# RG-LRU gates of a hybrid decoder step: high and low halves stacked in one operand, two products for each block of 64 channels instead of three for each gate

## The chip, the cores and the metric

The kernel runs on one core of a Trainium2 chip. The metric is the device time of one execution in microseconds (us). Engines are named as in the profile: PE (TensorE matmul; PEld is its weight load), DVE (VectorE), ACT (ScalarE), POOL (GpSimd), SP (SyncE, which issues loads). POOL issues the stores.

## The reference

One layer with two parallel head groups, for a prompt of 1024 tokens and for 8 decode rows. Both groups read one projection of the normalised input. What the change touches is the RG-LRU group's gates: the channels (1024) are cut into 16 blocks of 64, and each block has its own 64x64 weights.

```python
xc = conv_b + sum(conv_w[j] * ext[:, j:j + S] for j in range(CONV_W))
blocks = xc.reshape(B, S, NB_A, BW_A)                       # NB_A = 16, BW_A = 64
r = sigmoid(einsum('bsnc,ncd->bsnd', blocks, w_r) + b_r)
i = sigmoid(einsum('bsnc,ncd->bsnd', blocks, w_i) + b_i)
log_a = -LRU_C * r * softplus(-lam)
a = exp(log_a)
u = sqrt(-expm1(2.0 * log_a)) * (i * xc)
...                                                          # h = scan of (a, u) over the tokens
merged = concat[yA * silu(za), yB * silu(zb)]                # yB: mLSTM group
x = x + merged @ w_out
```

## The kernel before

Everything is float32. A product of float32 accuracy is made of parts: `split` writes a high half (a cast to the reduced format `fp32r`, on ACT) and a low half (source minus high, on DVE), and `mm3` adds three products, high by high, low by high and high by low, in one PSUM bank.

The program has three stretches. First the input is normalised, turned and split. Then the input projection runs over 14 units of column pairs (`UNITS`), each of 7 products (`Q_P1` to `Q_P4`, a Strassen-like scheme over 2x2 blocks), each product in two halves of 12 or 24 `mm3` products. Last come the mLSTM chunks (`m_a`, `m_b` ...) and the output projection.

Beside the projection runs a background: after each half product `pop_bg` takes steps from three lists, `bg` (gates' preparation, openings), `rgq` (RG-LRU, one step each time) and `dcq` (decode state). `rg_unit` puts a pair of column blocks into `rgq` once their `x` and `y` columns are stored: each column block `j` has 128 channels on the partitions and two halves `b` of 512 tokens, and `rg_half` gives the steps of one half, so there are 16 half blocks. A pair of column blocks is 4 half blocks and one load step. The last steps are `rg_final`, an empty one and `rg_rows`. When all lists are empty after the last q, k, v unit, `m_start` puts the mLSTM's first steps (`m_first`) into `bg`.

One half block before: `conv1` and `conv2` do the four taps on DVE and split the result `xc` into `xh` and `xl`; `gate_r` and `gate_i` each do one `mm3` on `xh`, `xl` with the weights `ghi`, `glo` of that gate and one tanh on ACT; `decay`, `scan` and `outs` follow on DVE and ACT. The weights stand in `graw` [128, 2, 128]: gate by gate, two 64x64 blocks on the diagonal, zeros elsewhere. Both gates' results go to the one PSUM bank with the tag `s`. The bank with the tag `tr` serves `dec_unit` alone at this time: 8 products of the decode rows and, a step later, their transposes. `rg_dec` does the same gates for the 8 decode rows with plain float32 products. `hb` holds half the biases, [channel, column block, gate].

The instruction order on each engine is made by a scheduler from the program's order and its own readiness estimates, so neighbours may change places.

Of the kernel before, what the change touches and what calls it, by code (L numbers as in the profile page):

```python
# [9 lines left out]
F32 = mybir.dt.float32  # L10
F32R = mybir.dt.float32r
BF16 = mybir.dt.bfloat16
AF = mybir.ActivationFunctionType
ALU = mybir.AluOpType
# [3 lines left out]
P = 128  # L18
T = 1024
HT = 512  # L20
NB = 8
# [8 lines left out]
R_CW, R_CB, R_BR, R_BI, R_LAM, R_GM, R_H0, R_CONV, R_N0, R_END = 0, 4, 5, 6, 7, 8, 9, 17, 41, 49  # L30
# [19 lines left out]
def hymba_kernel(  # L50
# [7 lines left out]
    V, A, G, TE = nc.vector, nc.scalar, nc.gpsimd, nc.tensor  # L58
    ld = nc.sync.dma_start
    stq = nc.gpsimd.dma_start  # L60

    def mm3(out, ah, al, bh, bl, first, last):

        TE.matmul(out, ah, bh, start=first, stop=False, skip_group_check=True)  # L64
        TE.matmul(out, ah, bl, start=False, stop=False, skip_group_check=True)  # L65
        TE.matmul(out, al, bh, start=False, stop=last, skip_group_check=True)  # L66

    def split(hi, lo, src):

        A.copy(hi, src)  # L70
        V.tensor_tensor(lo, src, hi.bitcast(F32), op=ALU.subtract)  # L71
# [7 lines left out]
    def ps(tag, shape):  # L79
        return psp.tile(shape, F32, tag=tag, name=f"ps_{tag}", bufs=NBUF.get(tag, 1))  # L80

    def const(shape, name, dt=F32):
        return cpool.tile(shape, dt, tag=name, name=name)
# [14 lines left out]
    def sg(shape, name, dt=F32):  # L98

        return stg.tile(shape, dt, tag="stg", name=name)  # L100
# [4 lines left out]
    def dconst(shape, name):  # L105

        return dpool.tile(shape, F32, tag=name, name=name)
# [10 lines left out]
    PT = dconst([P, KC, R_END], "PT")  # L118
# [5 lines left out]
    hb = const([P, KC, 2], "hb")  # L124
# [12 lines left out]
    dgr = dconst([P, 2, KC, NB], "dgr")  # L137
# [219 lines left out]
    fp = es_f.enter_context(tc.tile_pool(name="f_start", bufs=1))  # L357
# [161 lines left out]
    es_f = ExitStack()  # L519
    fp = es_f.enter_context(tc.tile_pool(name="f_gates", bufs=1, reuse_waits="tile"))  # L520

    def gates():

        par = ws([R_END, T], "par", F32)
# [22 lines left out]
        fx, ab, lg, z, z2, p = (gx[:, n, :] for n in range(6))  # L547
# [7 lines left out]
        lfd = lg[:, 32:64].rearrange("p (b h) -> p b h", h=NH)  # L555
        V.tensor_scalar(sp2, lg[:, 64:72], -2.0, None, op0=ALU.mult)
        V.tensor_scalar(sp4n, lg[:, 64:72], 4.0, None, op0=ALU.mult)
        V.tensor_scalar(hb, PT[:, :, R_BR:R_BR + 2], 0.5, None, op0=ALU.mult)
        V.tensor_scalar(gm4, PT[:, :, R_GM], 0.25, None, op0=ALU.mult)

        dgm = fp.tile([P, 2, NB, NH], F32, tag="dgm", name="dgm")
# [47 lines left out]
        for half in range(2):  # L609
            pk = ps(("s", "qp")[half], [P, 4, P])  # L610
            for q in range(4):
                c = half * 4 + q
                TE.transpose(pk[:, q, :], stk[:, c * P:(c + 1) * P], idF)
            s = slice(half * 4, half * 4 + 4)
# [20 lines left out]
    fpr = {}  # L635

    def rd_open():

        es_f.close()
        fpr["es"] = ExitStack()  # L640
        fpr["p"] = fpr["es"].enter_context(tc.tile_pool(name="f_rd", bufs=1, reuse_waits="tile"))
        fpr["graw"] = [fpr["p"].tile([P, 2, P], F32, tag=f"graw{i}", name=f"graw{i}") for i in range(2)]
        for t in fpr["graw"]:
            G.memset(t, 0.0)
        rg_gw(0)
        stq(s_conv[0, :, 0:2, :], st_conv[0, :, 1:3, :])
        dec_open()

    rst = {}
# [21 lines left out]
    def rg_unit(jj):  # L671
# [10 lines left out]
        if jj == 3:  # L682
            rgq.extend([rg_final, lambda: None, rg_rows])

    def rg_gw(j):
        if j < KC:
            graw = fpr["graw"][j % 2]
            for n, src in enumerate((w_rgate, w_igate)):
                for two in range(2):
                    s = slice(two * 64, two * 64 + 64)  # L690
                    ld(graw[s, n, s], src[0, 2 * j + two])

    def rg_half(j, b):
        fp = fpr["p"]
        pc = lambda r, n=1: PT[:, j, r:r + n]
        st = {}

        n = 2 * j + b

        def conv1():  # L700
            rg_load(n, True)
            xs = st["xs"] = rst["x", n]
            rg_load(n + 1)
            if b == 0:
                rg_gw(j + 1)
                ghi = fp.tile([P, 2, P], F32R, tag="ghi", name="ghi")
                glo = fp.tile([P, 2, P], F32R, tag="glo", name="glo")
                split(ghi, glo, fpr["graw"][j % 2])
                rst["g", j] = ghi, glo
            st["xc"] = xc = fp.tile([P, HT], F32, tag="xc", name="xc")  # L710
            V.tensor_scalar(xc, xs[:, 3:3 + HT], pc(R_CW + 3), pc(R_CB), op0=ALU.mult, op1=ALU.add)
            for t in (2, 1):
                V.scalar_tensor_tensor(xc, xs[:, t:t + HT], pc(R_CW + t), xc, op0=ALU.mult, op1=ALU.add)

        def conv2():
            xs, xc = st["xs"], st["xc"]
            V.scalar_tensor_tensor(xc, xs[:, 0:HT], pc(R_CW), xc, op0=ALU.mult, op1=ALU.add)
            st["xh"] = fp.tile([P, HT], F32R, tag="xh", name="xh")
            st["xl"] = fp.tile([P, HT], F32R, tag="xl", name="xl")
            split(st["xh"], st["xl"], xc)  # L720
            if b == 1:
                V.tensor_copy(OC[:, j, 1:4], xs[:, HT:HT + 3])

        def gate(g):
            ghi, glo = rst["g", j]
            pg = ps("s", [P, 512])
            mm3(pg, ghi[:, g, :], glo[:, g, :], st["xh"], st["xl"], True, True)
            return pg

        def gate_r():  # L730
            rg_load(n + 1, True)
            pg = gate(0)
            st["rg"] = fp.tile([P, HT], F32, tag="rg", name="rg")
            A.activation(st["rg"], pg, AF.Tanh, scale=0.5, bias=hb[:, j, 0:1])

        def gate_i():
            pg = gate(1)

            st["na"], st["ig"] = (fp.tile([P, HT], F32, tag=t, name=m) for m, t in (("na", "xh"), ("ig", "xl")))
            A.activation(st["ig"], pg, AF.Tanh, scale=0.5, bias=hb[:, j, 1:2])  # L740
            A.activation(st["na"], st["rg"], AF.Tanh, scale=sp2[:, j:j + 1], bias=sp2[:, j:j + 1])
            A.activation(st["rg"], st["rg"], AF.Exp, scale=sp4n[:, j:j + 1], bias=sp4n[:, j:j + 1])
            V.scalar_tensor_tensor(st["ig"], st["ig"], 1.0, st["xc"], op0=ALU.add, op1=ALU.mult)

        def decay():
            rg, na = st["rg"], st["na"]
            V.scalar_tensor_tensor(na, rg, 1.0, na, op0=ALU.add, op1=ALU.mult)
            V.tensor_scalar(rg, na, -1.0, 1.0, op0=ALU.mult, op1=ALU.add)
            V.scalar_tensor_tensor(na, na, 2.0, na, op0=ALU.subtract, op1=ALU.mult)
            A.activation(na, na, AF.Sqrt, scale=-0.25)  # L750

        def scan():
            rg, ig, na = st["rg"], st["ig"], st["na"]
            V.tensor_tensor(ig, ig, na, op=ALU.mult)
            V.tensor_tensor_scan(na, rg, ig, 0.0 if b == 0 else OC[:, j, 0:1], op0=ALU.mult, op1=ALU.add)
            V.tensor_copy(OC[:, j, 0:1], na[:, HT - 1:HT])

        def outs():
            na, zs = st["na"], rst["z", n]
            V.scalar_tensor_tensor(na, na, 0.5, zs, op0=ALU.mult, op1=ALU.mult)  # L760
            mh, ml = sg([P, HT], "rmh", F32R), sg([P, HT], "rml", F32R)
            split(mh, ml, na)
            stq(d_rm[0, j, :, b * HT:(b + 1) * HT], mh.bitcast(F32))
            stq(d_rm[1, j, :, b * HT:(b + 1) * HT], ml.bitcast(F32))
        return [conv1, conv2, gate_r, gate_i, decay, scan, outs]

    def rg_dec(j):

        pc = lambda r, n=1: PT[:, j, r:r + n]
        xc = dxc[:, j, :]  # L770
        cst = PT[:, j, R_CONV:R_CONV + 24].rearrange("p (b t) -> p b t", t=3)
        V.tensor_scalar(xc, dxz[:, 0, j, :], pc(R_CW + 3), pc(R_CB), op0=ALU.mult, op1=ALU.add)
        for t in range(3):
            V.scalar_tensor_tensor(xc, cst[:, :, t], pc(R_CW + t), xc, op0=ALU.mult, op1=ALU.add)
        pg = ps("s", [P, 2, NB])
        for g in range(2):
            TE.matmul(pg[:, g, :], fpr["graw"][j % 2][:, g, :], xc, start=g == 0, stop=True, skip_group_check=True)
        for g in range(2):
            A.activation(dgr[:, g, j, :], pg[:, g, :], AF.Tanh, scale=0.5, bias=hb[:, j, g:g + 1])

    def rg_final():

# [563 lines left out]
    def preps(n):  # L1346
        while state["prep"] < min(n, len(seq)):
            prep(*seq[state["prep"]])
            state["prep"] += 1

    gg = gates()
    bg.extend([lambda: next(gg, None)] * 17 + [rd_open])
    last_u = len(units) - 1
# [62 lines left out]
    for n in range(4, N):  # L1416
        c, h = n // 4, n % 4
# [90 lines left out]
```

## Time and profile before

| | us |
|---|---|
| median of 3 runs | 966.44 |
| the runs | 966.44, 966.21, 969.55 |
| the profiled execution | 970.22 |
| its span, first to last instruction | 968.1 |
| PE, DVE, ACT busy | 941.3, 697.4, 546.1 |
| gate products, first to last start | 143.8 to 535.8 |
| decode rows' gate products (L777), last start | 547.9 |

In rows of the profile, L12 is line 12 of the kernel. A group's row gives line, engine, operation, out<-in by the program's tile names, count, busy time, mean of one in ns, and idle time ahead of it with what ended it. `ps_s` is the PSUM tile of the tag `s`, `ps_tr` that of `tr`. In a row by tile, the three durations are least, median and greatest in ns, then first and last start. A timeline's row begins with start and duration in us. A row of waits gives who waited for whom, us in total, number and the longest.

### The profile page before, as it was taken

What the parts mean: (1) busy time and instruction counts of PE and PEld (TensorE: products, weight loads), DVE (VectorE), ACT (ScalarE), POOL (GpSimd) and SP (SyncE); (2) the same over time, 40 slices, a digit from 0 to 9 for tenths busy, and PEclk for the clock granted to TensorE, in tenths of its full rate; (3) what the DMA queues carried; (4) which work ended last, traced back from release to release, by engine and by line L of the source; (5) the groups of instructions that cost most, each with busy time, mean ns of one, the idle gap of its engine ahead of it and who ended that gap; (6) DMA issues with size and microseconds to landing.
All of it is one profiled execution on the core that took longest, in us unless ns stands there. A gap on an engine that the chain in (4) does not pass through costs nothing.

```text
span 968.1 us, 15367 instructions
## 1 busy us (share of the span) xinstructions
PE 941.3 (97%) x5402; PEld 768.4 (79%) x5402; DVE 697.4 (72%) x1447; ACT 546.1 (56%) x984; POOL 146.5 (15%) x260
## 2 busy tenths in 40 slices
PE   7999989999999999899999999999999999999997
PEld 7797767777787988687889898875667788888886
DVE  6775898988888877777786846686566677676764
ACT  6554456666666756454566744456546366465643
POOL 1111112121212122202212221010200100000020
PEclk9999999999999999999999999999999999999999
DMA  5431447356645455437645453424973754564481
GB/s 191 137 126 43 131 134 271 129 176 196 220 152 196 166 177 172 156 124 242 193 163 167 150 180 95 157 93 154 308 212 98 197 142 128 150 184 140 120 110 49
DMA packets 129314, 153.17 MB, mean 158 GB/s; under 512 B 13750, under 2 KB 107990, under 8 KB 129230
## 3 DMA queue, kind: packets, MB, share of 16 engines
q1 hardware_dynamic: 111510, 96.33, 33.8%
q0 software_dynamic: 17728, 55.87, 16.7%
q8 instruction: 42, 0.69, 0.3%
q14 instruction: 34, 0.28, 0.1%
HBM read 100.59 MB, written 51.65 MB: 157 GB/s over the span
## 4 chain that ended last, share of the span: by engine, by line
PE 43%; DMA 5%; DVE 5%; issue 4%; ACT 1%; POOL 0%; SPq 0%; DVEq 0%; POOLq 0%; ACTq 0%
PE ps_o L66 7%; PE ps_o L64 7%; PE ps_o L65 7%; PE ps_kv L64 5%; PE ps_kv L65 5%; PE ps_kv L66 5%; DMA W<-d_alpha 3%; PE ps_tr L227 1%; PE ps_s L1058 1%; DVE Cl L71 1%; PE ps_qp L64 1%; DVE Cf L1119 1%; DMA rh<-d_rm 1%; PE ps_qp L65 1%; PE ps_qp L66 1%
## 5 line engine op out<-in xcount | busy, mean ns | idle before, releaser
L70 ACT CAST wh<-raw 128x1024 fp32r<-128x1024 f32 x91 | 95.5, 1050 | 74.7 <-PE ps_o L65 24.5
L71 DVE TENSOR_TENSOR wl<-raw,wh 128x1024 fp32r<-128x1024 f32 x91 | 110.9, 1218 | 31.6 <-ACT wh L70 19.4
L64 PE MATMUL ps_kv<-cb_hi,wh 128*128 128x512 f32 x320 | 129.0, 403 | 0.1
L66 PE MATMUL ps_kv<-cb_hi,wl 128*128 128x512 f32 x320 | 126.1, 394 | 0.0
L65 PE MATMUL ps_kv<-cb_lo,wh 128*128 128x512 f32 x320 | 125.9, 393 | 0.0
L64 PE MATMUL ps_o<-cb_hi,wh 128*128 128x512 f32 x240 | 94.7, 394 | 0.0
L66 PE MATMUL ps_o<-cb_hi,wl 128*128 128x512 f32 x240 | 93.9, 391 | 0.0
L65 PE MATMUL ps_o<-cb_lo,wh 128*128 128x512 f32 x240 | 93.7, 390 | 0.0
L64 PEld LDWEIGHTS ps_kv<-cb_hi,wh 128*128 128x128 f32 x320 | 60.4, 189 | 24.8 <-issue 5.5
L66 PEld LDWEIGHTS ps_kv<-cb_hi,wl 128*128 128x128 f32 x320 | 60.5, 189 | 15.7 <-issue 2.5
L65 PEld LDWEIGHTS ps_kv<-cb_lo,wh 128*128 128x128 f32 x320 | 60.6, 189 | 11.9
L66 PE MATMUL ps_o<-wo,ml 128*128 128x512 f32 (+1 forms) x136 | 52.2, 384 | 3.2 <-DVE ml L71 3.1
L64 PE MATMUL ps_kv<-wh,cb_hi 128*128 128x256 f32 x192 | 55.3, 288 | 0.0
L65 PE MATMUL ps_kv<-wl,cb_hi 128*128 128x256 f32 x192 | 54.3, 283 | 0.0
L66 PE MATMUL ps_kv<-wh,cb_lo 128*128 128x256 f32 x192 | 54.3, 283 | 0.0
L64 PE MATMUL ps_o<-wo,rh 128*128 128x512 f32 (+1 forms) x136 | 53.9, 397 | 0.0
L64 PEld LDWEIGHTS ps_o<-cb_hi,wh 128*128 128x128 f32 x240 | 45.1, 188 | 10.8 <-issue 1.7
L66 PEld LDWEIGHTS ps_o<-cb_hi,wl 128*128 128x128 f32 x240 | 45.0, 188 | 10.3 <-issue 0.8
L64 PE MATMUL ps_o<-wo,mh 128*128 128x512 f32 (+1 forms) x136 | 52.9, 389 | 0.0
L65 PE MATMUL ps_o<-wo,rh 128*128 128x512 f32 (+1 forms) x136 | 52.3, 384 | 0.0
L65 PEld LDWEIGHTS ps_o<-cb_lo,wh 128*128 128x128 f32 x240 | 45.1, 188 | 9.0
L66 PE MATMUL ps_o<-wo,rl 128*128 128x512 f32 (+1 forms) x136 | 52.1, 383 | 0.0
(469 smaller groups left out, 2506.9 us busy)
## 6 DMA issues: line engine op xcount, KB each, us to landing
raw<-in_w_in_dram SPq DMA_DIRECT2D x56, 512.0 KB
Cb<-in_state_mlstm_C_dram SPq DMA_DIRECT2D x32, 256.0 KB
out_dram<-Cb POOLq DMA_DIRECT2D x32, 256.0 KB, 4.6
qk<-d_qk SPq DMA_DIRECT2D x32, 256.0 KB
oraw<-in_w_out_dram SPq DMA_DIRECT2D x16, 512.0 KB
d_qk<-s POOLq DMA_DIRECT2D x24, 256.0 KB, 4.2
x<-in_x_prompt_dram SPq DMA_DIRECT2D x8, 512.0 KB
d_x<-s POOLq DMA_DIRECT2D x16, 256.0 KB, 2.9
```

Of the source, the lines that this page charges most:

```text
L64: TE.matmul(out, ah, bh, start=first, stop=False, skip_group_check=True)
L65: TE.matmul(out, ah, bl, start=False, stop=False, skip_group_check=True)
L66: TE.matmul(out, al, bh, start=False, stop=last, skip_group_check=True)
L70: A.copy(hi, src)
L71: V.tensor_tensor(lo, src, hi.bitcast(F32), op=ALU.subtract)
L227: TE.matmul(pz[32 * g:32 * g + 32, :], hnd[:, k, :], raws[u, k // 4][:, k % 4, :], start=k < 4, stop=k >= 4, skip_group_check=True)
L1058: TE.matmul(S, qk[:, 2 + kb, :], qk[:, kb, :], start=kb == 0, stop=kb == 1)
L1119: V.scalar_tensor_tensor(mx["Cf"][h][:, kb, :], mx["Cf"][h][:, kb, :], cs_b[:, h, c:c + 1], kvs[kb], op0=ALU.mult, op1=ALU.add)
```

## The change

- `graw` is filled otherwise: both 64-row halves hold the same weights, and the free index runs over the block first (0 or 1), with the r gate's 64 columns and the i gate's 64 behind it. It is now full, so its two clearing memsets go.
- The input has two operands instead of `xh` and `xl`: operand `n` has the high half of block `n` on that block's own 64 partitions and the low half on the other 64. Four instructions of 64 partitions write them: two casts on ACT in `conv2`, two differences on DVE in a step of their own, `lows`, between `conv2` and the first gate step.
- A product of operand `n` with the stacked weights gives (high + low) times the high weights, for both gates at once: r on the lower 64 partitions of the bank, i on the upper 64. A second adds the low weights. So there are two products for each block and four for a half block, where there were six; the product of low by low comes in addition.
- Block 0 goes to the bank `s`, block 1 to the bank `tr`.
- `gate_out` takes a block's bank apart: tanh of its lower half into the block's 64 partitions of `rg`, tanh of its upper half into those of `ig`. That is four tanh of 64 partitions for a half block instead of two of 128. `hb` is stored to match.
- `rg_dec` does the same: the two halves of `xc` are copied into `dxs`, whose other halves are zero, and there are four small tanh instead of two.
- A half block has 8 steps instead of 7.

```diff
-        V.tensor_scalar(hb, PT[:, :, R_BR:R_BR + 2], 0.5, None, op0=ALU.mult)
+        for n, s in enumerate(LOHI):
+            for m, d in enumerate(LOHI):
+                V.tensor_scalar(hb[d, :, n], PT[s, :, R_BR + m], 0.5, None, op0=ALU.mult)
...
-        for t in fpr["graw"]:
-            G.memset(t, 0.0)
+        fpr["dxs"] = fpr["p"].tile([P, 2, NB], F32, tag="dxs", name="dxs")
+        G.memset(fpr["dxs"], 0.0)
...
+    def gate_out(rg, ig, pg, j, n):
+        for m, t in enumerate((rg, ig)):
+            A.activation(t[LOHI[n]], pg[LOHI[m]], AF.Tanh, scale=0.5, bias=hb[LOHI[m], j, n:n + 1])
...
-                for two in range(2):
-                    s = slice(two * 64, two * 64 + 64)
-                    ld(graw[s, n, s], src[0, 2 * j + two])
+                for s in LOHI:
+                    ld(graw[s, :, n * 64:n * 64 + 64], src[0, 2 * j:2 * j + 2].rearrange("t c d -> c t d"))
...
-            split(st["xh"], st["xl"], xc)
+            st["xx"] = [fp.tile([P, HT], F32R, tag=t, name=t) for t in ("xh", "xl")]
+            for n, s in enumerate(LOHI):
+                x = st["xx"][n]
+                A.copy(x[s], xc[s])
...
+        def lows():
+            for n, s in enumerate(LOHI):
+                x = st["xx"][n]
+                V.tensor_tensor(x[LOHI[1 - n]], st["xc"][s], x[s].bitcast(F32), op=ALU.subtract)
+
+        def gate(n):
+            pg = ps(("s", "tr")[n], [P, 512])
+            for k, w in enumerate(rst["g", j]):
+                TE.matmul(pg, w[:, n, :], st["xx"][n], start=k == 0, stop=k == 1)
             return pg
...
-        return [conv1, conv2, gate_r, gate_i, decay, scan, outs]
+        return [conv1, conv2, lows, gate_a, gate_b, decay, scan, outs]
...
+        for n, s in enumerate(LOHI):
+            V.tensor_copy(dxs[s, n, :], xc[s])
```

`gate_a` and `gate_b` each call `gate` for one block and `gate_out` on its bank; `gate_b` then does what `gate_i` did behind its tanh.

The order that results is shown at three places. The first is PE in the first half block of column block 0. Before, the first gate product stands between two projection products, and the low half's product three projection products later:

```order
L66 MATMUL ps_o<-cb_hi_160,wl_2_1477 128x512
L64 MATMUL ps_s<-xh,ghi 128x512
L64 MATMUL ps_kv<-cb_hi_162,wh_3_1547 128x512
L65 MATMUL ps_kv<-cb_lo_163,wh_3_1547 128x512
L66 MATMUL ps_kv<-cb_hi_162,wl_3_1548 128x512
L65 MATMUL ps_s<-xl,ghi 128x512
L66 MATMUL ps_s<-xh,glo 128x512
```

Changed, the same half block has its pairs here:

```order
L65 MATMUL ps_kv<-cb_lo_163,wh_3_1550 128x512
L742 MATMUL ps_s<-xh,ghi 128x512
L742 MATMUL ps_s<-xh,glo 128x512
L66 MATMUL ps_kv<-cb_hi_162,wl_3_1551 128x512
L742 MATMUL ps_tr<-xl,ghi 128x512
L742 MATMUL ps_tr<-xl,glo 128x512
```

The first product has moved behind projection products of the next product, and each pair reads one operand that already holds high and low.

The second place is DVE in the same half block, from the last tap to the next weights' low half (`Cb` is the decode state, `wl` a projection weight's low half). Before:

```order
L717 SCALAR_TENSOR_TENSOR xc<-xs,PT,xc 128x512
L722 COPY OC<-xs 128x3
L873 SCALAR_TENSOR_TENSOR Cb<-vbc,kw,Cb 128x256
L660 MEMSET xs 128x3
L873 SCALAR_TENSOR_TENSOR Cb<-vbc,kw,Cb 128x256
L71 TENSOR_TENSOR xl<-xc,xh 128x512
L873 SCALAR_TENSOR_TENSOR Cb<-vbc,kw,Cb 128x256
L71 TENSOR_TENSOR wl_5_1647<-raw_2_1331,wh_5_1646 128x1024
```

Changed:

```order
L725 SCALAR_TENSOR_TENSOR xc<-xs,PT,xc 128x512
L890 SCALAR_TENSOR_TENSOR Cb<-vbc,kw,Cb 128x256
L664 MEMSET xs 128x3
L890 SCALAR_TENSOR_TENSOR Cb<-vbc,kw,Cb 128x256
L736 TENSOR_TENSOR xh<-xc,xh 64x512
L736 TENSOR_TENSOR xl<-xc,xl 64x512
L890 SCALAR_TENSOR_TENSOR Cb<-vbc,kw,Cb 128x256 x2
L71 TENSOR_TENSOR wl_5_1648<-raw_2_1334,wh_5_1647 128x1024
```

Where one difference of 128 partitions stood, two of 64 stand one behind the other.

The third is PE around the decode rows' products (L227) and their transposes (L235) that follow the second half block, changed:

```order
L742 MATMUL ps_tr<-xl,ghi 128x512
L742 MATMUL ps_tr<-xl,glo 128x512
...
L64 MATMUL ps_kv<-cb_hi_156,wh_0_1735 128x512
L227 MATMUL ps_tr<-raw_3_1596,hnd 32x512 x4
L227 MATMUL ps_tr<-raw_3_1690,hnd 32x512 x4
...
L235 MATMUL ps_tr<-idF,Z 128x128 x4
```

Seven projection products stand between the second block's pair and the decode rows' products in the same bank; before, no gate product used that bank.

More of the change, by code (lines that the diff above doesn't have):

```diff
@@ L520, in hymba_kernel @@
     fp = es_f.enter_context(tc.tile_pool(name="f_gates", bufs=1, reuse_waits="tile"))
+    LOHI = slice(0, 64), slice(64, 128)
     def gates():
@@ L717, in conv2, with gate_a, gate_b @@
             V.scalar_tensor_tensor(xc, xs[:, 0:HT], pc(R_CW), xc, op0=ALU.mult, op1=ALU.add)
-            st["xh"] = fp.tile([P, HT], F32R, tag="xh", name="xh")
-            st["xl"] = fp.tile([P, HT], F32R, tag="xl", name="xl")
-            split(st["xh"], st["xl"], xc)
+            st["xx"] = [fp.tile([P, HT], F32R, tag=t, name=t) for t in ("xh", "xl")]
+            for n, s in enumerate(LOHI):
+                x = st["xx"][n]
+                A.copy(x[s], xc[s])
             if b == 1:
                 V.tensor_copy(OC[:, j, 1:4], xs[:, HT:HT + 3])
[L724 to L727, printed above, removed]
+        def lows():
[6 more added lines that the diff above has]
+                TE.matmul(pg, w[:, n, :], st["xx"][n], start=k == 0, stop=k == 1)
             return pg
-        def gate_r():
+        def gate_a():
             rg_load(n + 1, True)
             pg = gate(0)
-            st["rg"] = fp.tile([P, HT], F32, tag="rg", name="rg")
-            A.activation(st["rg"], pg, AF.Tanh, scale=0.5, bias=hb[:, j, 0:1])
-        def gate_i():
+            st["rg"], st["ig"] = (fp.tile([P, HT], F32, tag=t, name=m) for m, t in (("rg", "rg"), ("ig", "xh")))
+            gate_out(st["rg"], st["ig"], pg, j, 0)
+        def gate_b():
             pg = gate(1)
-            st["na"], st["ig"] = (fp.tile([P, HT], F32, tag=t, name=m) for m, t in (("na", "xh"), ("ig", "xl")))
-            A.activation(st["ig"], pg, AF.Tanh, scale=0.5, bias=hb[:, j, 1:2])
+            gate_out(st["rg"], st["ig"], pg, j, 1)
+            st["na"] = fp.tile([P, HT], F32, tag="xl", name="na")
             A.activation(st["na"], st["rg"], AF.Tanh, scale=sp2[:, j:j + 1], bias=sp2[:, j:j + 1])
@@ L774, in rg_dec @@
             V.scalar_tensor_tensor(xc, cst[:, :, t], pc(R_CW + t), xc, op0=ALU.mult, op1=ALU.add)
+        dxs = fpr["dxs"]
+        for n, s in enumerate(LOHI):
+            V.tensor_copy(dxs[s, n, :], xc[s])
         pg = ps("s", [P, 2, NB])
[L776 to L779, printed above, removed]
+        for n in range(2):
+            TE.matmul(pg[:, n, :], fpr["graw"][j % 2][:, n, :], dxs[:, n, :], start=n == 0, stop=True, skip_group_check=True)
+        for n in range(2):
+            gate_out(dgr[:, 0, j, :], dgr[:, 1, j, :], pg[:, n, :], j, n)
     def rg_final():
```

## The prediction

> **What bounds the kernel now.** I read the page's engine shares first, then the busy time in stretches, then TensorE's list of waits, then the timeline around those waits.
>
> ```profile
> PE 941.3 (97%) x5402; PEld 768.4 (79%) x5402; DVE 697.4 (72%) x1447; ACT 546.1 (56%) x984; POOL 146.5 (15%) x260
> 200.00:260.00 60.00, 59.21 (x286) 45.03 (x283) 48.74 (x81) 38.77 (x54) 14.34 (x25) 1.00 0.69 222
> 260.00:320.00 60.00, 60.00 (x325) 47.37 (x324) 52.45 (x87) 40.15 (x57) 10.26 (x18) 1.00 0.49 163
> 380.00:440.00 60.00, 57.47 (x260) 44.80 (x259) 43.05 (x71) 31.96 (x44) 10.66 (x18) 0.97 0.47 156
> 552.00:640.00 88.00, 88.00 (x580) 76.70 (x579) 54.91 (x112) 45.77 (x83) 12.10 (x20) 1.00 0.43 134
> ```
>
> The columns after the length are PE, PEld, DVE, ACT and POOL, then clock, DMA share and GB/s. PE is full wherever the RG-LRU gates run (140 to 550 us), DVE comes next (52.45 of 60 us in its fullest stretch), ACT has a third free. One row is short of full and short of clock: 380 to 440 us.
>
> ```profile
> PE ps_s L64 <- ACT xh L70: 2.3, 3, 1.4
> PE ps_s L65 <- DVE xl L71: 1.9, 2, 1.1
> PE ps_s L64 <- ACT rg L734: 0.7, 1, 0.7
> ```
>
> These are all the waits of PE between 138 and 552 us, and each is a gate product: five for the two halves of the convolved input, one for the bank `ps_s`, which the r gate had not left.
>
> A busy PE is not yet what a product costs, because each record overlaps the next. The start times give that.
>
> ```profile
> 147.76 0.39 PE L64 MATMUL ps_s<-xh,ghi 128*128 128x512 f32 x1
> 147.99 0.39 PE L65 MATMUL ps_s<-xl,ghi 128*128 128x512 f32 x1
> 148.21 0.40 PE L66 MATMUL ps_s<-xh,glo 128*128 128x512 f32 x1
> 148.45 0.39 PE L64 MATMUL ps_kv<-cb_hi,wh 128*128 128x512 f32 x1
> ```
>
> Three gate products take 148.45 - 147.76 = 0.69 us, so 0.23 us each, not the 0.39 of the record. Whoever prices by the record's length nearly doubles the gain.
>
> **Part 1: fewer products.** Each of the 16 half blocks (8 channel blocks by 2 halves) had two gates of three products; it gets two products for each of two blocks of 64 channels, 4 instead of 6. The low-by-low product comes in with no product of its own. That is 32 fewer at 0.23 us: -7.4 us, all on the engine that is the path.
>
> **Part 2: the waits of the gates.** Before, `conv2` issued the last tap, ACT's cast and DVE's difference in a row, and the r gate stood one background step later.
>
> ```profile
> 384.33 0.88 DVE L873 SCALAR_TENSOR_TENSOR Cb<-vbc,kw,Cb 128x256 f32<-128x256 f32 x2 [4.42 <-DMA vbc<-d_dv]
> 398.66 0.61 ACT L70 CAST xh<-xc 128x512 fp32r<-128x512 f32 x1
> 399.33 0.50 PE L64 MATMUL ps_s<-xh,ghi 128*128 128x512 f32 x1 [1.43 <-ACT xh L70]
> 400.18 0.68 DVE L71 TENSOR_TENSOR xl<-xc,xh 128x512 fp32r<-128x512 f32 x1
> 400.92 0.50 PE L65 MATMUL ps_s<-xl,ghi 128*128 128x512 f32 x1 [1.09 <-DVE xl L71]
> 401.49 0.61 PE L64 MATMUL ps_kv<-cb_hi,wh 128*128 128x512 f32 x1
> 404.88 0.41 PE L66 MATMUL ps_kv<-cb_hi,wl 128*128 128x512 f32 x1
> 402.00:404.00 2.00, 2.00 (x6) 1.55 (x5) 0.00 (x0) 0.40 (x1) 0.00 (x0) 0.50 0.16 59
> ```
>
> Here is the largest: DVE waits 4.42 us for a decode vector, is late for the rest of the block, and PE stands for the cast and then for the difference. After that the granted clock is 0.50: the 8 products from 401.49 to 404.88 took 0.42 us each, 8 x (0.42 - 0.23) = 1.5 us more. In all the gates wait 2.3 + 1.9 + 0.7 = 4.9 us. A wait is counted from the end of the record ahead, which overlaps by 0.39 - 0.23 = 0.16, so six waits cost 4.9 + 6 x 0.16 = 5.9 us, and with the clock 7.4 us.
>
> Now the casts stay in `conv2`, the differences are a step of their own, `lows`, and the first products come a step after that: one more step, which is 12 products of 0.23 = 2.8 us of PE. That exceeds the longest wait of 1.43 us. The second block's products go to `ps_tr`, so they do not wait until ACT has left `ps_s`. Bounds: all 7.4 us may go, or none, if the new waits of Part 4 are as long. I take 5.4 us gone and 2.0 us left, near the first end, because the wait at 399 us with its clock is over half of the total and comes from ACT and DVE working one behind the other right ahead of the product; the new step parts these.
>
> The Trainium skill, "TensorE: Matmul & The Clock Gate", section "Why this matters for your kernels", asks only that idle gaps between bursts stay under some 3 us. By that rule gaps like these would cost themselves alone and the sum would lose the 1.5 us. The trace disagrees: two waits, 1.43 and 1.09 us with a product between, were followed by half clock.
>
> **Part 3: more work on ACT and DVE.** Half as many partitions do not make an instruction shorter; the trace before has the comparison.
>
> ```profile
> L580 ACT COPY rows<-ps_qp x2: 571/573/575, 86.2 to 89.0; 4x512 f32<-4x512 f32 x2
> L305 ACT COPY s<-ps_o 128x512 f32<-128x512 f32 x26 | 15.2, 583 | 22.4 <-PE ps_o L66 22.3
> L605 DVE TENSOR_TENSOR stk<-rows,gsm x1: 1218/1218/1218, 127.7 to 127.7; 4x1024 f32<-4x1024 f32 x1
> L71 DVE TENSOR_TENSOR wl<-raw,wh 128x1024 fp32r<-128x1024 f32 x91 | 110.9, 1218 | 31.6 <-ACT wh L70 19.4
> L734 ACT ACTIVATE rg<-ps_s,hb x16: 667/687/698, 146.6 to 532.5; 128x512 f32<-128x512 f32 x16
> L70 ACT CAST xh<-xc x16: 603/618/626, 143.2 to 530.2; 128x512 fp32r<-128x512 f32 x16
> L71 DVE TENSOR_TENSOR xl<-xc,xh x16: 678/684/693, 145.1 to 530.9; 128x512 fp32r<-128x512 f32 x16
> L779 ACT ACTIVATE dgr<-ps_s,hb x16: 259/267/272, 178.1 to 549.2; 128x8 f32<-128x8 f32 x16
> 143.07 0.16 DVE L722 COPY OC<-xs 128x3 f32<-128x3 f32 x1
> ```
>
> Four partitions cost ACT 573 ns against 583 for 128, and DVE 1218 against 1218, the latter while it writes 64 partitions further on, as `lows` will. So a half block costs ACT one more cast (0.618) and two more tanh (2 x 0.687): 1.99 us, 31.9 us over 16. The decode gates cost two more of 0.267 for each of 8 blocks: 4.3 us. DVE gets 16 x 0.684 = 10.9 us, 16 small copies of about 0.16 for `dxs` (2.6 us, estimated from L722), and three more short ones for `hb`, about 0.5 us by the same row. Together ACT +36, DVE +14 us.
>
> None of it is on the path while PE covers it. A background list gives out one RG-LRU step for each half product, 14 for each pair of column blocks; each RG-LRU pair now has 33 steps instead of 29, so the list, 119 steps before, has 135. The same work is spread over more time: DVE does about 10 us for 7 steps now and 10.7 for 8 then, so its load for each step falls. If that cover were gone, the price would be the 14 us of DVE.
>
> The list ends some 5 half products later, and with it begin the mLSTM's first steps (`m_first`). They still end ahead of the output weights' preparation, under a stretch where PE is at 88.00 of 88.00, DVE at 54.91 and ACT at 45.77; I cost the shift at nothing. `outs` and its two stores on POOL, the x and z loads and the next block's gate loads on SP move with their steps; their readers come behind the projection's end.
>
> ```profile
> L691 SPq DMA_DIRECT2D graw<-in_w_rgate_dram x16: 471/569/597, 130.8 to 418.1; - x16
>   DMA graw<-in_w_igate_dram: 2.1, 1
> ```
>
> The gate weights keep their 32 loads; each now carries 128 pieces of 256 bytes instead of 64, because both row halves are filled. They were waited for once (2.1 us, by ACT) and are asked for a whole block ahead: nothing. Two memsets on POOL become one, smaller. ACT's table loads stay at 53 in the instruction order; those at L734 come up at the new function instead.
>
> **Part 4: new waits.** Three: (a) the first products wait for `lows` on DVE; behind them on PE stand all projections. (b) `ps_tr` now serves the decode rows' products, their transposes and the second block. Ahead of one decode group there are 7 projection products (7 x 0.23 = 1.6 us), in which ACT must do two tanh (1.4 us) and whatever is queued; short by about 1 us there and at two similar places. (c) the decode gates' products wait for two more copies, 8 x 0.32 = 2.6 us if nothing covers. Bounds 0 and 16 x 0.684 + 3 + 2.6 = 16.5 us; this is the 2.0 us that Part 2 leaves, near the lower end, since the waits on DVE for the same kind of work were 1.9 us.
>
> **The sum.** The profiled execution took 970.22 us (span 968.1): 970.2 - 7.4 - 5.4 = 957.4. It lies 3.8 us above the median of the runs, 966.44; the runs 966.21, 966.44 and 969.55 suggest that the wait at 399 us (1.43 + 1.09 + 2 x 0.16 + 1.5 = 4.3 us) is not in every execution. Without it the sum is 966.4 - 7.4 - 3.1 + 2.0 = 957.9; 3.1 are the other waits. Both say 957.5.
>
> **Rivals.**
> - A, above: products and most waits go. 957.5, of itself 953 to 960. Chance 0.60.
> - B: the products go, the waits only change place (the list of waits shows DVE queues of several us, which one step does not outlast): 966.4 - 7.4 = 959.0, to 961. Chance 0.18.
> - C: `ps_tr` or the decode gates' copies stop PE at most decode groups: 13 groups at about 0.4 us give back 5 us, 964. For it speaks how near the users of that bank stand; against it that PE never waited for `ps_tr` after 140 us. Chance 0.14.
> - D, the other side: DVE becomes the bound at `lows`. Two differences, 1.37 us, stand in DVE's queue at the moment when PE's next half product covers 2.8 us, and DVE is at 52.45 of 60 there. It turns into a loss when each of 16 half blocks waits 7.4 / 16 = 0.46 us longer than now; at 1.37 us each it is 966.4 - 7.4 + 21.9 - 5 = 976. Against it: the step's own 2.8 us. Chance 0.05.
> - E: the products go but PE was not the path, because a later stage waits for DMA that is issued by its own clock: 966. Against it: the output stage's loads are issued by the same program order. Chance 0.03.
>
> **Numbers.** A change under 0.5% (4.8 us) can hardly be told from none here. Faster by more means under 961.6: A, B and a little of C, 0.81. Within 0.5%: most of C, E, part of D, 0.15. Slower: 0.04. The range, 952.0 to 962.5, reaches from all waits gone (966.4 - 7.4 - 7.4 = 951.6) to C's better half.
>
> **What would show it.** Right: 64 gate products at 0.23 us where 96 stood; no wait of PE for `xh` over 1 us; half-partition tanh at about 0.69 us; ACT near 582 and DVE near 711 us busy; no dip of the clock between 380 and 440 us. Wrong: PE waits for DVE's `xh` or `xl` in many half blocks (D), for ACT at `ps_tr` (C), or an execution whose output stage is longer than before (E).

## The result and the profile after

| | before | changed |
|---|---|---|
| median of 5 runs, us | 967.14 | 960.78 |
| the runs, us | 966.21 to 969.55 | 958.7 to 962.3 |
| the profiled execution (its span), us | 970.22 (968.1) | 958.7 (956.9) |

The ratio of the times is 0.9922, 95% interval 0.9900 to 0.9944: 7.5 us faster, with an interval from 5.4 to 9.7 us. The medians alone differ by 6.4 us. The forecast was 957.5 us.

The changed kernel's engine shares, then its busy times in stretches, with the columns of the same rows before.

```profile
PE 930.1 (97%) x5370; PEld 761.9 (80%) x5370; DVE 713.1 (75%) x1482; ACT 586.9 (61%) x1048; POOL 146.2 (15%) x259
```

```profile
200.00:260.00 60.00, 59.95 (x297) 45.05 (x295) 52.96 (x89) 44.38 (x63) 14.11 (x24) 1.00 0.66 220
260.00:320.00 60.00, 60.00 (x346) 49.51 (x343) 54.21 (x90) 42.92 (x61) 10.46 (x18) 1.00 0.48 162
380.00:440.00 60.00, 60.00 (x292) 45.58 (x290) 53.09 (x88) 43.92 (x64) 11.60 (x20) 1.00 0.55 184
552.00:640.00 88.00, 88.00 (x547) 75.16 (x546) 60.72 (x128) 51.00 (x93) 12.25 (x21) 1.00 0.43 137
```

PE has 32 matmuls fewer. The stretch at 380 us, short of 2.53 us and of clock before, is full at clock 1.00. ACT and DVE have 40.8 and 15.7 us more to do, and PE stays full beside them.

The waits of PE between 138 and 552 us, changed kernel (who waited for whom, us, times, longest):

```profile
PE ps_kv L64 <- ACT s L308: 3.5, 3, 1.8
PE ps_s L742 <- DVE xh L736: 1.9, 2, 1.6
```

Here lies the surprise. The gates' waits fell from 4.9 to 1.9 us, but a place that never waited before has 3.5 us: a projection product that needs the bank `ps_kv`, which ACT has to empty (`s`, L308). In sum 4.9 became 5.4 us. The timeline of the longest of them, ACT and PE:

```profile
466.31 0.72 ACT L888 ACTIVATE Cb<-Cb,dGI 128x512 f32<-128x512 f32 x1 [5.26 <-DMA out_dram<-Cb]
467.05 0.58 ACT L308 COPY s<-ps_kv 128x512 f32<-128x512 f32 x1
467.69 0.50 PE L64 MATMUL ps_kv<-cb_hi,wh 128*128 128x512 f32 x1 [1.79 <-ACT s L308]
```

ACT stands 5.26 us ahead of the scaling of the decode state (`A.mul(C, C, dGI)`, tile `Cb`), whose buffer comes free only when an earlier state has been stored. The evacuation of `ps_kv` is the next instruction in ACT's queue, so it stands too, and PE with it.

For the comparisons below two measures are worked out from the traces. *Stopped*: between 138 and 560 us, for each projection and gate product the time to the next start on PE as far as it exceeds the undisturbed pitch (0.228 us for 512 columns, 0.120 for 256), and PE's idle time ahead of such a product where it follows one of another kind, summed; it holds waits, half clock and joints. One to two microseconds of it are jitter that every kernel has, so it serves to compare kernels. *Stretch*: from the first decode product (L227) of unit 2 to that of unit 11 (units counted from 0), in which nearly all half blocks lie.

| kernel | median, us | ratio [95%] | stretch, us | stopped, us |
|---|---|---|---|---|
| before | 967.14 | 1 | 421.5 | 16.8 |
| changed | 960.78 | 0.9922 [0.9900, 0.9944] | 411.1 | 14.8 |
| `put_back` | 967.3 | 0.9992 [0.9969, 1.0015] | 418.2 | 15.0 |
| `step_alone` | 964.74 | 0.9956 [0.9936, 0.9976] | 415.2 | 12.1 |
| `no_step` | 966.26 | 0.9981 [0.9961, 1.0001] | 416.7 | 19.2 |
| `one_bank` | 961.01 | 0.9919 [0.9888, 0.9950] | 410.6 | 13.4 |
| `half_tanh` | 979.93 | 1.0124 [1.0091, 1.0158] | 433.2 | 23.2 |
| `step_half` | 976.12 | 1.0071 [1.0046, 1.0097] | 426.9 | 22.5 |
| `step_pieces` | 977.08 | 1.0086 [1.0058, 1.0113] | 428.1 | 22.7 |
| `step_two` | 961.46 | 0.9920 [0.9896, 0.9943] | 411.5 | 15.0 |
| `pool_mul` | 968.5 | 1.0009 [0.9987, 1.0031] | 416.4 | 20.2 |
| `late_cast` | 964.02 | 0.9955 [0.9932, 0.9978] | 413.0 | 16.3 |
| `dve_mul` | 961.35 | 0.9928 [0.9912, 0.9944] | 409.9 | 14.0 |
| `late_scale` | 958.7 | 0.9912 [0.9888, 0.9936] | 408.9 | 12.8 |

Each ratio is to the kernel before in runs on the same chip; the medians come from several chips, so kernels are compared by their ratios. Intervals are some 0.25% to either side, so two kernels that differ by less than about 3 us are not told apart by their times; stretch and stopped time are of one execution of each.

### The profile page after: what moved, and what is told of

The parts are those of the page before. It is cut to its first block, busy times and chain, and to the rows that moved or that the text cites. A ratio compares the mean times of both kernels' runs of the same rounds, so it can differ in the third digit from the quotient of the medians.

```text
span 956.9 us, 15419 instructions
## 1 busy us (share of the span) xinstructions
PE 930.1 (97%) x5370; PEld 761.9 (80%) x5370; DVE 713.1 (75%) x1482; ACT 586.9 (61%) x1048; POOL 146.2 (15%) x259
## 3 DMA queue, kind: packets, MB, share of 16 engines
q0 software_dynamic: 17728, 55.87, 16.3%
## 4 chain that ended last, share of the span: by engine, by line
PE 71%; DVE 10%; DMA 8%; issue 5%; ACT 4%; SPq 1%; POOL 0%; DVEq 0%; ACTq 0%; POOLq 0%
PE ps_o L66 12%; PE ps_o L64 11%; PE ps_o L65 11%; PE ps_kv L64 8%; PE ps_kv L66 8%; PE ps_kv L65 8%; PE ps_tr L227 2%; DMA W<-d_alpha 2%; DMA Cb<-in_state_mlstm_C_dram 2%; PE ps_s L1075 1%; DMA out_dram<-Cb 1%; DVE wl L71 1%; DMA x<-in_x_prompt_dram 1%; PE ps_qp L64 1%; PE ps_tr L1211 1%
## 5 line engine op out<-in xcount | busy, mean ns | idle before, releaser
L64 PE MATMUL ps_kv<-cb_hi,wh 128*128 128x512 f32 x320 | 128.2, 401 | 3.5 <-ACT s L308 3.5
L71 DVE TENSOR_TENSOR wl<-raw,wh 128x1024 fp32r<-128x1024 f32 x91 | 111.2, 1222 | 27.2 <-ACT wh L70 16.8
L64 PE MATMUL ps_o<-cb_hi,wh 128*128 128x512 f32 x240 | 95.0, 396 | 0.0
L64 PEld LDWEIGHTS ps_kv<-cb_hi,wh 128*128 128x128 f32 x320 | 60.1, 188 | 26.8 <-ACT s L308 4.5
L64 PE MATMUL ps_kv<-wh,cb_hi 128*128 128x256 f32 x192 | 55.4, 288 | 0.0
L64 PEld LDWEIGHTS ps_o<-cb_hi,wh 128*128 128x128 f32 x240 | 45.1, 188 | 10.7 <-issue 1.7
L64 PE MATMUL ps_o<-wo,rh 128*128 128x512 f32 (+1 forms) x136 | 53.4, 393 | 0.0
L64 PE MATMUL ps_o<-wo,mh 128*128 128x512 f32 (+1 forms) x136 | 52.8, 388 | 0.0
```

## The experiments

**The products: `put_back`.** The changed kernel with 96 gate products again; the first product of each block is done twice.

```diff
-            for k, w in enumerate(rst["g", j]):
-                TE.matmul(pg, w[:, n, :], st["xx"][n], start=k == 0, stop=k == 1)
+            ghi, glo = rst["g", j]
+            for k, w in enumerate((ghi, ghi, glo)):
+                TE.matmul(pg, w[:, n, :], st["xx"][n], start=k < 2, stop=k == 2, skip_group_check=True)
```

> The changed kernel with the first product of each block done twice (the second writes over the first): 6 products a half block as before, 32 more in all. Both theories: 32 x 0.23 = 7.4 us over the changed kernel, about 968. The rival that PE is not the path there: 961.

0.9992 against 0.9922: 0.70%, 6.8 us. The stretch is 418.2 - 411.1 = 7.1 us longer, and stopped time is nearly the same (15.0 and 14.8). So the 32 products cost what 32 x 0.23 = 7.4 says, within the error of some 3 us, and PE is the path.

**The step: `step_alone` and `no_step`.** The kernel before with the step `lows` alone, and the changed kernel without it (`lows()` at the end of `conv2`).

```diff
-            split(st["xh"], st["xl"], xc)
+            A.copy(st["xh"], xc)
...
+        def lows():
+            V.tensor_tensor(st["xl"], st["xc"], st["xh"].bitcast(F32), op=ALU.subtract)
...
-        return [conv1, conv2, gate_r, gate_i, decay, scan, outs]
+        return [conv1, conv2, lows, gate_r, gate_i, decay, scan, outs]
```

> The kernel before, with only the new step: the difference (one instruction of 128 partitions) is a background step of its own between conv2 and gate_r; three products a gate, bank and tanh as before. Theory 1 (the gates' waits were worth some 4 us and went with the step; the added work of ACT gave as much back): 3 to 5 us under the kernel before, about 963. Theory 2 (the gates' waits fall on few executions, the step is worth nothing): within 1 us of the kernel before, 967.

> The changed kernel with the differences put back into conv2, so 7 steps for a half block again; products, banks and tanh as changed. Theory 1: 3 to 5 us over the changed kernel, about 964.5, with waits of PE for DVE at the gate products. Theory 2: within 1 us of the changed kernel, 961.

`step_alone` gains 0.44% (4.3 us), `no_step` loses 0.59% (5.7 us) against the changed kernel. The longest waits of PE between 138 and 560 us, `no_step` first, then `step_alone`:

```profile
PE ps_s L743 <- DVE xh L737: 5.3, 6, 1.4
PE ps_tr L743 <- DVE xl L737: 1.6, 2, 1.4
PE ps_kv L64 <- ACT s L308: 1.4, 2, 0.7
```

```profile
PE ps_kv L64 <- ACT s L308: 2.1, 2, 1.5
PE ps_s L64 <- ACT xh L720: 1.0, 1, 1.0
```

Without the step PE waits for the differences in eight places, with it the gates' waits nearly go. But in `step_alone` too, with none of the changed kernel's other edits, `ps_kv` has begun to wait for ACT: the later order by itself is enough to bring that wait. It isn't needed for it, since `no_step` has 1.4 us of the same wait without the step.

**The bank: `one_bank`.** Both blocks in bank `s`.

```diff
-            pg = ps(("s", "tr")[n], [P, 512])
+            pg = ps("s", [P, 512])
```

> The changed kernel with both blocks' products in the bank s. Theory 1: the second block waits for the first's two tanh at some of the 16 places, 0.5 us each, and one decode group is split: 2 to 5 us over the changed kernel, 963 to 966. Rival (the bank tr itself is what costs, by meeting the decode rows): 2 to 3 us under it, 958.

0.9919 against 0.9922, between the two expectations: the second bank neither helps nor hurts by more than the error of some 3 us. PE never waits at `ps_tr` in the changed kernel's list above, so the trace shows no loss there either.

**The pieces: `half_tanh`, `step_half`, `step_pieces`.** Half-partition instructions in the kernel before: its two tanh cut into four; the same with the step `lows`; and that with cast and difference cut too. The edit to the tanh:

```diff
-            A.activation(st["rg"], pg, AF.Tanh, scale=0.5, bias=hb[:, j, 0:1])
+            for s in (slice(0, 64), slice(64, 128)):
+                A.activation(st["rg"][s], pg[s], AF.Tanh, scale=0.5, bias=hb[s, j, 0:1])
```

> The kernel before, with each of the two gate tanh cut into two of 64 partitions: 32 more instructions of about 0.69 us, 22 us more work on ACT and nothing else. Theory 1: part of the 4 us given back shows here, 2 to 4 us over the kernel before, about 970, with PE waiting for ACT at evacuated banks. Theory 2: ACT has room, 967.

> The kernel before with the new step and, on top, each gate tanh cut into two of 64 partitions (22 us more on ACT). Theory 1, now: the step gives ACT's delay cover, so the cut tanh cost a few us and not the 12 that they cost without the step: 2 to 4 us over the kernel with the step alone, about 967; one decode group of PE is split by a gate product, which is 1 us of it. Rival (ACT's work costs the same with the step): 12 us over it, about 977.

> As the kernel with step and cut tanh, with the casts and the differences cut into two of 64 partitions too: all the additional instructions of the change, with the products and the bank of before. If products, step and pieces add up, it lies 7.4 us over the changed kernel, about 968, and the pieces have eaten the step. Rival (the pieces cost nothing, the bank tr takes the step's gain back): 964, as the kernel with the step alone.

`half_tanh` loses 1.24% (12 us), three times the most that was expected, and the step does not cover it: `step_half` and `step_pieces` stand 1.15 and 1.30% above `step_alone`, the first as its rival said, the second outside both expectations. The tanh alone is what counts; cutting cast and difference as well adds 0.15%, inside the error. Yet it isn't the amount of work: `put_back` does the same cut instructions and the same 96 products as `step_pieces` and is 0.94% (9 us) faster. Stopped time says so too, 15.0 against 22.7 us. One stop of `step_half`, ACT and PE:

```profile
307.62 0.72 ACT L876 ACTIVATE Cb<-Cb,dGI 128x512 f32<-128x512 f32 x1 [6.96 <-DMA Cb<-in_state_mlstm_C_dram]
309.18 1.37 ACT L738 ACTIVATE rg<-ps_s,hb 64x512 f32<-64x512 f32 x2
310.61 0.79 PE L64 MATMUL ps_s<-xh,ghi 128*128 128x512 f32 x1 [2.29 <-ACT rg L738]
```

It is the changed kernel's pattern again: ACT stands for the decode state, and the next tanh, which frees the bank, stands behind it and one weight cast, now as two instructions of together 1.37 us. In `half_tanh` about half of the loss is of another kind. PE, from 173 us:

```profile
173.34 1.05 PE L227 MATMUL ps_tr<-raw,hnd 128*32 128x512 f32 x2
174.32 0.50 PE L64 MATMUL ps_s<-xh,ghi 128*128 128x512 f32 x1
174.65 0.39 PE L65 MATMUL ps_s<-xl,ghi 128*128 128x512 f32 x1
174.88 0.40 PE L66 MATMUL ps_s<-xh,glo 128*128 128x512 f32 x1
175.21 1.49 PE L227 MATMUL ps_tr<-raw,hnd 128*32 128x512 f32 x11
```

The view ends in the last row; 14 products of the group follow the gate's three. The scheduler put a gate's products into the middle of the decode rows' group, which is otherwise run in one piece. It did so in five units. A whole group takes 1.33 us from its first to its last start; four of the split ones took 3.19 and one 3.85, of which three gate products are 0.69: 1.2 us lost in each of four, 1.8 in the fifth. Of the 433.2 - 421.5 = 11.7 us, stopped time accounts for 6.4 and these joints, most of which that measure leaves out, for the rest.

**The change without its pieces: `step_two`.** The kernel before with the step and with two products for each gate, whole instructions and one bank. Left out is the low weights' product.

```diff
-            mm3(pg, ghi[:, g, :], glo[:, g, :], st["xh"], st["xl"], True, True)
+            TE.matmul(pg, ghi[:, g, :], st["xh"], start=True, stop=False, skip_group_check=True)
+            TE.matmul(pg, ghi[:, g, :], st["xl"], start=False, stop=True, skip_group_check=True)
```

> The kernel before with the step `lows` and with two products for each gate (64 where 96 stood), but with whole instructions: casts, differences and tanh stay at 128 partitions, and every gate stays in bank `s`. Left out is the product of the high input by the low weight, so the low part of the gate weights isn't used. It is the change without its half-partition pieces. Theory 1 (the two gains add up, and the pieces gave some of it back in the changed kernel): from 967.1, less 7 for the products and 4.3 to 5 for the step, 955 to 956.5, ratio 0.988 to 0.989. Theory 2 (the pieces cost nothing in the changed kernel; the products and the step overlap, each saving the same waits): like the changed kernel, 960.8, ratio 0.993. Over 963 both fall.

0.9920, like the changed kernel's 0.9922. So the cut instructions cost the changed kernel nothing that can be measured. Products (0.70%) and step (0.44%) would add up to 0.9886; that sum has an error of its own of some 0.3%, so the times do not settle whether the two gains add up. The trace speaks against it: compared with `step_alone` stopped time rose from 12.1 to 15.0 us, and one stop has about as much. ACT, then PE:

```profile
297.76 0.72 ACT L875 ACTIVATE Cb<-Cb,dGI 128x512 f32<-128x512 f32 x1 [7.97 <-DMA Cb<-in_state_mlstm_C_dram]
298.38 1.03 ACT L70 CAST wh<-raw 128x1024 fp32r<-128x1024 f32 x1
299.32 0.68 ACT L738 ACTIVATE rg<-ps_s,hb 128x512 f32<-128x512 f32 x1
300.05 0.50 PE L730 MATMUL ps_s<-xh,ghi 128*128 128x512 f32 x1 [2.75 <-ACT rg L738]
```

The same pattern at a third place.

**Which of ACT's stands matters: `late_cast`.** ACT's largest wait for DVE in the changed kernel is at `rmh` (14.7 us, 13 times). Here that cast, its difference and its stores come one and two steps later.

```diff
-            mh, ml = sg([P, HT], "rmh", F32R), sg([P, HT], "rml", F32R)
-            split(mh, ml, na)
...
+            def cast():
+                mh, ml = sg([P, HT], "rmh", F32R), sg([P, HT], "rml", F32R)
+                A.copy(mh, na)
...
+            pend.append(cast)
```

> The changed kernel with the cast of `outs` (`rmh`) put off into the next half block's `conv1`, and its difference and stores into the next `conv2`; no step is added, nothing is left out. ACT waited there for DVE 13 times, 14.7 us, and what stands behind it in ACT's queue (casts, tanh, evacuations of the mLSTM) waited too. Theory 1 (ACT's standing in its queue is what gives back part of the gain): these waits fall under 5 us and the time falls by 2 to 4 us against the changed kernel, 957 to 959, ratio 0.990 to 0.992. Rival (the waits at `rmh` are idle time of an engine with slack and only move): 960 to 962, ratio 0.993 to 0.995.

The ratio is 0.9955, some 3 us slower than the changed kernel, which is just the size of the error, and outside both expectations. The waits at `rmh` only went from 14.7 to 12.7 us, not under 5, so the edit did not do what it was made for and says little about `rmh`. Those for the decode state's load rose from 7.0 to 17.8, while the one of 5.26 us for its store went. The longest stop, ACT, then PE:

```profile
298.84 0.72 ACT L905 ACTIVATE Cb<-Cb,dGI 128x512 f32<-128x512 f32 x1 [6.08 <-DMA Cb<-in_state_mlstm_C_dram]
...
304.68 0.68 ACT L692 ACTIVATE ig<-ps_tr,hb 64x512 f32<-64x512 f32 x1
305.41 2.47 PE L227 MATMUL ps_tr<-raw,hnd 128*32 128x512 f32 x16 [2.85 <-ACT ig L692]
```

and the clock behind it, in two stretches:

```profile
306.00:308.00 2.00, 2.00 (x17) 0.32 (x6) 1.93 (x5) 1.91 (x4) 0.24 (x1) 0.66 0.59 216
308.00:310.00 2.00, 2.00 (x10) 2.00 (x11) 2.00 (x4) 0.80 (x2) 0.00 (x0) 0.50 0.03 8
```

ACT stood 6.08 us, was then busy without a gap, and the second block's last tanh left `ps_tr` late for the decode products: rival C's place, by another cause. Then the granted clock went to 0.66 and 0.50.

**The scaling on another engine: `pool_mul` and `dve_mul`.** The changed kernel, with

```diff
-                A.mul(C, C, dGI[:, b, h:h + 1])
+                G.tensor_scalar(C, C, dGI[:, b, h:h + 1], None, op0=ALU.mult)
```

and with `V.tensor_scalar` in the same place.

> The changed kernel with the decode state's scaling (32 instructions of 128x512, 0.72 us each) moved from ACT to POOL. If ACT, which stands in its order behind that state's loads and has 36 us more to do, gives back what the step gained, taking 23 us and those waits from it brings 3 to 4 us: 957. If ACT's load costs nothing: 961; if POOL then holds the stores up, more than 961.

> The changed kernel with the decode state's scaling on DVE in place of ACT (`V.tensor_scalar`), so that ACT never waits for the state's load; nothing is left out. DVE reads the same tile right after, so it waits there in any case. DVE gets 32 more instructions, which no row here prices (a 128x512 difference took 0.684 us; 32 of these would be 22 us). Theory 1 (ACT's standing in its queue is what stops PE): ACT's waits for the load are gone, PE's waits for ACT at `ps_kv` go with them, 957 to 960, ratio 0.990 to 0.993. Rival (DVE is the engine with the least to spare in this stretch, 52 to 54 of 60 us): PE's waits for DVE grow, 962 to 968, ratio 0.995 to 1.001, as when POOL had the scaling.

The scaling on POOL (least, median, greatest ns), and from the list of waits what waits for it and PE's two longest beside that for `xh`:

```profile
L888 POOL TENSOR_SCALAR Cb<-Cb,dGI x32: 1552/1575/3638, 136.3 to 538.4; 128x512 f32<-128x512 f32 x32
```

```profile
DVE Cb L890 <- POOL Cb L888: 15.1, 8, 3.0
PE ps_tr L235 <- ACT Z L230: 2.8, 3, 1.9
PE ps_tr L227 <- ACT ig L692: 2.0, 1, 2.0
```

The same two for DVE:

```profile
L888 DVE TENSOR_SCALAR Cb<-Cb,dGI x32: 470/482/490, 143.2 to 533.7; 128x512 f32<-128x512 f32 x32
```

```profile
PE ps_s L742 <- DVE xh L736: 3.6, 3, 2.1
```

On POOL the scaling takes 1575 ns where ACT took 724, DVE waits for it, PE waits 9.7 us in all where it waited 5.4, and the gain is gone (1.0009). That the one brings the other, by way of DVE's and ACT's later work, is argued and not traced step by step. On DVE the scaling takes 482 ns; PE no longer waits for ACT at `ps_kv`, but for `xh` on DVE 3.6 us instead of 1.9, its longest 2.1, and 0.9 us at `ps_tr`: 4.5 us in all. The ratio, 0.9928, lies in the first expectation's range (0.990 to 0.993) and is not told apart from the changed kernel's. Most of the wait only changed engines.

**The state given longer to land: `late_scale`.** The changed kernel; for the first token of each pair scaling, sums and store come one half product (2.8 us) later. Nothing else is moved.

```diff
-                A.mul(C, C, dGI[:, b, h:h + 1])
...
+                def update():
+                    A.mul(C, C, dGI[:, b, h:h + 1])
...
+                if b % 2:
+                    update()
+                else:
+                    late.append(update)
```

> The changed kernel with one edit outside the gates: for the first token of each pair the update of the decode state (ACT's scaling `A.mul(C, C, dGI)`, DVE's two sums, the store) is put off by one half product, 2.8 us, so that the state's load has that much longer to land. Amounts of work are the same, nothing is left out. Theory 1 (the stops that are left come from ACT standing for the state's load, with an evacuation behind it in its queue: 5.26 us at 466 us in the changed kernel, 7.97 us at 298 us in `step_two`, 6.08 us at 299 us in `late_cast`, each with PE stopped for 1.8 to 2.8 us after it): ACT's longest wait at the scaling falls under 3 us, PE has no wait over 2 us between 138 and 560 us, and the time falls by 2 to 3 us against the changed kernel, 957.5 to 959, ratio 0.990 to 0.991. Rival (any other order finds a stop of its own): 960 to 962, ratio 0.993 to 0.995, with a wait of 1.5 to 3 us at another place.

958.7 us, 0.9912, the lowest of all kernels here. The waits of PE between 138 and 560 us, and ACT's two at the scaling, first here, then in the changed kernel:

```profile
PE ps_kv L64 <- ACT s L308: 1.6, 2, 1.1
PE ps_s L742 <- DVE xh L736: 1.6, 2, 1.3
ACT Cb L890 <- DMA Cb<-in_state_mlstm_C_dram: 10.1, 9, 2.8
ACT Cb L890 <- DMA out_dram<-Cb: 3.5, 1, 3.5
```

```profile
ACT Cb L888 <- DMA Cb<-in_state_mlstm_C_dram: 7.0, 8, 1.6
ACT Cb L888 <- DMA out_dram<-Cb: 5.3, 1, 5.3
```

The 5.26 us at 466 us became 3.5, the wait at `ps_kv` fell from 3.5 to 1.6 us, no wait of PE is longer than 1.3 us, and the stretch is 2.2 us shorter. That is what the theory says, by its mechanism; the expected "under 3 us" on ACT was missed by half a microsecond. In sum ACT waits no less for the state than before the edit, 13.6 us against 12.3: what shrank is the longest stand and the stop of PE behind it. The times alone do not show a gain, since the intervals of 0.9912 and 0.9922 overlap. By its trace, this form of the changed kernel is the one to take.

## Why the prediction held, and which of its terms did not

- **The gain by the times** was forecast at 966.4 - 957.5 = 8.9 us and came out at 7.5, with an interval from 5.4 to 9.7. The times alone do not show that the forecast was off; what follows on its terms rests on the traces, one execution of each kernel.
- **The products (-7.4) held**: 6.8 us by the times of `put_back`, 7.1 by its stretch. That PE is the path held with it; rival E falls.
- **The waits (5.4 gone, 2.0 left) is the step that failed.** The half that the prediction looked at went as described: the stopped time ahead of gate products fell from 7.2 to 3.1 us, the wait at 399 us is gone with its half clock, and `no_step` shows that the step does it. But that ahead of projection products at L64 rose from 1.6 to 4.4 us, and in sum stopped time fell from 16.8 to 14.8, by 2.0 and not 5.4. From the profiled execution: 970.2 - 7.4 - 2.0 = 960.8; measured 958.7. The 2 us between are in the output stage: from the last unit's first decode product to the end it is 331.7 us before and 329.7 changed. There the execution of before had a dip of the clock and that of the changed kernel had none. The same 16 us of it, before and then changed:

```profile
700.00:716.00 16.00, 14.18 (x67) 9.82 (x65) 10.06 (x20) 7.43 (x15) 0.00 (x0) 0.89 0.78 238
```

```profile
700.00:716.00 16.00, 15.94 (x85) 11.71 (x86) 11.96 (x30) 7.87 (x19) 0.55 (x1) 1.00 0.70 195
```

  Such a dip, between 680 and 732 us, stands in every other profile here but that of `step_pieces`, so most executions probably pay it: the median of the changed kernel is 960.78 where its profiled execution was 958.7. So it is in part luck that the profiled execution came within 1.3 us of the sum's 957.4: the waits gave 3.4 us less than forecast, and the missing dip, which the prediction had not asked for, gave 2.0 back.
- **What was not asked**: Part 4 listed three new waits, all at the gates. The queue that mattered was ACT's, which has the gates' casts and tanh, the evacuations of the projection and the scaling of the decode state in one order; in four of the orders tried (the changed kernel, `step_half`, `step_two`, `late_cast`) another of them stood behind a state that had not landed or whose buffer had not been stored. Part 3 looked at how much ACT has to do and at its free third; how long it stands, and with what behind it, was not looked at, though ACT waited 20.5 us for that state in the kernel before, where it did not yet stop PE at `ps_kv`:

```profile
ACT Cb L871 <- DMA Cb<-in_state_mlstm_C_dram: 20.5, 13, 4.2
```

- **Part 3's nothing for the pieces** holds in the changed kernel within the error (`step_two`), with ACT at 586.9 us (582 forecast) and DVE at 713.1 (711). It does not hold in the kernel before, where the cut tanh cost 12 us. Why one order meets so many more stops than the other is not settled: the traces name the stops, and no run isolates what places them.
- **Rival B had the number too**, 959.0 to 961: the products go, the waits only change place. Its mechanism was half right. They changed place, but to ACT's queue and not to DVE's, and not all of them. Rival C's bank cost nothing that can be measured (`one_bank`), and in the changed kernel's trace no decode gate product waits for the copies; waits of PE at its place, decode products behind ACT at `ps_tr`, turned up in `late_cast` and `pool_mul`, with 2.8 and 2.0 us, and with 0.5 us or less in `no_step` and `put_back`. D did not come: PE waits for the differences 1.9 us in all.
- Of the signs named, the 0.23 us pitch, half tanh of 683 ns and the clear stretch at 380 us came; "no wait for `xh` over 1 us" did not quite, with one of 1.6 us at 146 us, where the RG-LRU list begins. The half tanh by line, and a first pair of products in the timeline:

```profile
L692 ACT ACTIVATE rg<-ps_s,hb x16: 667/683/687, 147.0 to 543.0; 64x512 f32<-64x512 f32 x16
```

```profile
296.25 0.39 PE L742 MATMUL ps_s<-xh,ghi 128*128 128x512 f32 x1
296.48 0.39 PE L742 MATMUL ps_s<-xh,glo 128*128 128x512 f32 x1
296.71 0.39 PE L64 MATMUL ps_kv<-cb_hi,wh 128*128 128x512 f32 x1
```

## What to carry to other kernels

Work taken off the engine that is the path came back at its pitch here, within the error (7.1 us by the stretch for 7.4); a wait taken away came back only so far as no other queue stood in its place. Before a gain from waits is booked, list the waits of every engine that frees banks for the path, a load in its queue above all, and ask what stands behind each: what shortened the stops here was not at the gates but 2.8 us more for a load. And changes to an order are worth what the trace of the new order shows; two gains measured one by one (0.70% and 0.44%) gave 0.8% together, though with errors of this size the times alone do not exclude their sum.

## What the runs showed of the hardware

- Cutting a tanh by partitions doubles its cost: 683 ns for 64 partitions, 687 for 128; casts 620 and 618, differences 685 and 684.
- The scaling of a 128x512 tile took 482 ns on DVE, 724 on ACT and 1575 on POOL.
- A stop of PE is paid a second time only in some cases. After 2.85 us in `late_cast` the granted clock was 0.50 and products of 256 columns took 0.21 instead of 0.12 us for some 3 us; after 2.75 us in `step_two` it stayed at 1.00:

```profile
300.00:302.00 2.00, 1.95 (x8) 1.61 (x9) 1.82 (x4) 2.00 (x4) 0.67 (x1) 1.00 0.46 153
302.00:304.00 2.00, 2.00 (x15) 1.18 (x17) 1.97 (x4) 1.97 (x4) 1.30 (x2) 1.00 0.51 163
```

  The Trainium skill, "TensorE: Matmul & The Clock Gate", section "Why this matters for your kernels", asks for gaps under some 3 us between bursts. Both stops are under that; one was followed by half clock, the other, only 0.1 us shorter, was not. The kernel before had half clock after stops of 1.43 and 1.09 us, and the changed kernel none after one of 1.79, so in these traces the length of the last gap alone does not decide. What does was not tried.
- Decode products of 32 columns of weights, run as a group, lose time where other products are put between them: in `half_tanh` two of them took until the next start 0.98 us, and a group of 16 split in this way took 1.2 us longer than the 1.33 us of a whole one and the 0.69 us of the three products put into it.
